# Latent attention: the order of the first value product, a two-bank value projection, and the rotated query's copies

## The chip, the cores and the metric

The kernel runs on one core of one Trainium2 chip. Its engines work side by side, each in its own order: TensorE (PE in the profile; its weight loads are PEld), VectorE (DVE), ScalarE (ACT), GpSimd (POOL) and SyncE (SP), which issues the transfers. The metric is the device time of one execution in microseconds; the time before is the median of three runs.

## The reference

Two layers of a decoder trunk over 512 tokens of width 1024, in float32. Each layer normalises its input, projects it once, and feeds three branches: a state-space scan (SSD), multi-head latent attention (MLA), and a gated delta network (GDN). Their outputs are gated, projected, and followed by a feed-forward block. The change lies in the MLA branch, whose core is, cut to what matters:

```python
q = (rmsnorm(cq, q_norm_g) @ w_uq).reshape(Bsz, S, H, MLA_NOPE + MLA_ROPE)   # 8 heads, 128 + 64
q_nope, q_pe = jnp.split(q, [MLA_NOPE], axis=-1)
q_pe = apply_rope(q_pe, ...)
kv = (rmsnorm(ckv, kv_norm_g) @ w_ukv).reshape(Bsz, S, H, MLA_NOPE + MLA_V)
k_nope, v = jnp.split(kv, [MLA_NOPE], axis=-1)
k_pe = apply_rope(k_rope, cos, sin)          # one rotated key of 64, shared by all heads
scale = (128 + 64) ** -0.5
# per block of 128 queries: scores = (q_nope . k_nope + q_pe . k_pe) * scale, causal,
# softmax over the keys, then the product with v
```

## The kernel before

Every large product is made of three matmuls on values split in two: a rounded high part (`h`) and the rest, the low part (`l`); high times high, high times low, low times high. ACT rounds the high part (L270, `split_act`), and DVE subtracts it from the source to get the low part (L271). Weights are split the same way (L170 on ACT, L171 on DVE) as they arrive. A scheduler sets the order on every engine from its own estimate of when operands are ready; products of later work ("fillers") are put between the steps of a head that wait for another engine. Results stand in eight PSUM banks of 128x512: four `acc`, three `sm`, one `yt`.

The attention takes the eight heads in four pairs (`hp`), two heads (`j`) in each:

- L589 to L608: the query weights are loaded and split, and the query product gives three banks: the plain queries of the two heads, and one bank with the rotated 64 columns of both (64 partitions each). For the first pair the third bank is `yt`.
- L610 to L627: the queries are split; the rotated part is scaled into `qp` and rotated by `rope` (L545 to L554). That makes a swapped copy by four transfers of 32 partitions (L549), then two products and a sum on DVE (L551 to L553).
- L629 to L636: the rotated query is needed twice over the 128 partitions, since its partner `kps` holds the high half of the rotated key in the first 64 partitions and the low half in the last 64. Two transfers of 64 partitions (L630) make a copy `qd` with the halves swapped. For each head ACT rounds its own half (L634) and the other half from `qd` (L636) into `qps[j]`, and DVE makes the low part `qpl[j]` (L635). The other half of `qpl[j]` is zeroed once (L585), so that it can be multiplied with the whole of `kph`.
- L637 to L639: key/value weights and the key product, `k`, two banks.
- L641 to L656: the value product for both heads, tokens on the partitions, into four `acc` banks of 128x256, one for each block of 128 tokens. Each bank is read out in two halves of 128x128, by ACT and by DVE.
- L658 to L681, for each head and each block `t` of 128 queries: five matmuls of scores (L667 to L671; L670 takes `qps`, L671 `qpl` with `kph`), then the softmax: DVE L676, ACT L678, DVE L679 and L680, into `pn`.
- L682 to L706: the probabilities are transposed on PE by key block `kb` (L688), split into `th` and `tl`, and multiplied into `po` (bank `yt`): L704 high values with `th`, L705 high values with `tl`, L706 low values with `th`. For `kb` 0, `th` and `tl` are 512 wide.
- L708: the head's output is split.

At the start of the branch L561 to L568 rotate the shared key and make `kph` and `kps`; `latent` (L274 on ACT, L275 on DVE) normalises and splits the latent `ckh`, `ckl`.

Of the kernel before, what the change touches and what calls it, by code (L numbers as in the profile page):

```python
# [10 lines left out]
F32 = mybir.dt.float32  # L11
# [44 lines left out]
def hybrid_kernel(ctx, tc, a, out, depth=2, taps=None):  # L56
# [4 lines left out]
    def mk(pl, shape, dt, tag, bufs=None):  # L61
        return pl.tile(shape, dt, tag=tag, name=f"{tag}_{next(uid)}", bufs=bufs)
# [5 lines left out]
    def f32(ap):  # L68
        return ap.bitcast(F32)
# [198 lines left out]
    def split_act(hi, lo, src):  # L268
        with tc.high_priority(30):
            act.copy(hi, src)  # L270
            dve.tensor_tensor(lo, src, f32(hi), ALU.subtract)  # L271
# [113 lines left out]
    for ly in range(depth):  # L385
# [177 lines left out]
        kpe = rope(kd)  # L563
        kph = mk(ml, [P, S], F32R, "kph")
        kps = mk(ml, [P, S], F32R, "kps")
        act.copy(kph, kpe)
        act.copy(kps[:64], kpe[:64])
        dve.tensor_tensor(kps[64:], kpe[64:], f32(kph[64:]), ALU.subtract)  # L568

# [10 lines left out]
        for x in pts:  # L580
            pool.memset(f32(x[:, :P]), 0.0)

        qpl = [mk(ml, [P, S], F32R, f"qpl{j}") for j in range(2)]
        for j in range(2):
            pool.memset(f32(qpl[j][64 * (1 - j) : 64 * (1 - j) + 64]), 0.0)  # L585

        scale = (128 + 64) ** -0.5
        yh, yl = [None] * KD, [None] * KD
        for hp in range(4):  # L589
# [37 lines left out]

            qd = mk(lp, [P, S], F32, "mix", 8)
            for i in range(2):  # L629
                sync.dma_start(qd[64 * i : 64 * i + 64], qr[64 * (1 - i) : 64 * (1 - i) + 64])  # L630
            qps = [mk(ml, [P, S], F32R, f"qps{j}") for j in range(2)]
            for j in range(2):
                half, other = (slice(64 * i, 64 * i + 64) for i in (j, 1 - j))
                act.copy(qps[j][half], qr[half])  # L634
                dve.tensor_tensor(qpl[j][half], qr[half], f32(qps[j][half]), ALU.subtract)  # L635
                act.copy(qps[j][other], qd[other])  # L636
            wkv = list(weights(a["mla_w_ukv"][ly], hp * 512, 512, 256))  # L637
# [4 lines left out]
            for j in range(2):  # L642
                if hp % 2 == 0:
                    v2 = [mk(ml, [P, S], F32R, nm, 2) for nm in ("vh", "vl")]
                elif hp == 1:
                    v2 = [mk(lp, [P, S], F32R, f"y{e}{6 + j}") for e in "hl"]
                else:
                    v2 = [mk(ml, [P, S], F32R, f"cq{e}{j}") for e in "hl"]
                vs.append([x.rearrange("p (t n) -> p t n", t=T) for x in v2])

            def ev(t, ps):
                for j in range(2):
                    split_act(*(x[:, t, :] for x in vs[j]), ps[:, j * P : (j + 1) * P])

            vcols = lambda w: w.rearrange("p (h n) -> p h n", h=2)[:, :, P:]
            dense_T(wkv, 256, 256, ckh, ckl, ev, vcols)  # L656

            for j in range(2):  # L658
# [3 lines left out]
                for t in range(T):  # L662
# [7 lines left out]
                    pe.matmul(o, qps[j][:, tok], kps[:, :n], start=False, stop=False)  # L670
                    pe.matmul(o, qpl[j][:, tok], kph[:, :n], start=False, stop=True)  # L671
                    n = (t + 1) * P
# [10 lines left out]
                for kbs in ((0,), (1,), (3, 2)):  # L683
# [16 lines left out]
                    for kb, c0, c in parts:  # L700
                        v_h, v_l = (x[:, kb, :] for x in vs[j])
                        o = po[:, c0:]
                        w = S - c0
                        pe.matmul(o, v_h, th[:, c : c + w], start=kb == 0, stop=False)  # L704
                        pe.matmul(o, v_h, tl[:, c : c + w], start=False, stop=False)  # L705
                        pe.matmul(o, v_l, th[:, c : c + w], start=False, stop=kb == T - 1)  # L706
# [800 lines left out]
```

## Time and profile before

| | us |
|---|---|
| median of three runs | 2264.68 (2264.63 to 2265.31) |
| the profiled execution, its own time | 2266.44 |
| its span | 2264.7 |
| PE busy | 2250.4 (99%) |
| DVE busy | 1648.5 (73%) |
| ACT busy | 1185.7 (52%) |
| POOL busy | 64.7 (3%) |

The granted clock of PE is 0.999 of full speed. The span is what the trace covers; the execution's own time has a little more around it. Times inside the trace count from the start of the span. The attention of the first layer lies at 58 to 210 us, that of the second at 1180 to 1340 us. A row of a timeline gives start, duration, engine, line, operation, written tile and read tiles, and shape; brackets give the idle time of the engine ahead of it and what ended it. An `x2` joins two operations.

### The profile page before, as it was taken

To read this page: it belongs to the slowest core of one execution; us is meant where nothing else is said; L and a number is where in the kernel's file an instruction comes from. 1 tells how busy PE (TensorE), PEld (TensorE's weight loads), DVE (VectorE), ACT (ScalarE), POOL (GpSimd) and SP (SyncE) were. 2 spreads that over 40 slices of the span, in tenths; PEclk is the share of its full clock that TensorE was granted. 3 is DMA by queue.
4 is the path that set the end of the run, shared out by engine and by line. 5 is a ranking of instruction groups with operands and counts; after the bars stand their busy time and mean duration, and the time that the engine had idled before them with its cause. 6 is when DMAs were issued, how large, how long until landed. Compare 5 with 4: busy or idle time off the path is not lost.

```text
span 2264.7 us, 32107 instructions
## 1 busy us (share of the span) xinstructions
PE 2250.4 (99%) x11758; PEld 1866.1 (82%) x11758; DVE 1648.5 (73%) x3315; ACT 1185.7 (52%) x2448; POOL 64.7 (3%) x84
## 2 busy tenths in 40 slices
PE   9999999999999999999999999999999999999998
PEld 8888787888888888888888887888888888888887
DVE  7886567876767778767878865678758668778668
ACT  6665644333543555554656667443335435645546
POOL 1000000000000000000010000000001000000000
PEclk9999999999999999999999999999999999999999
DMA  4223633452225143233132236345422251432231
GB/s 144 82 75 104 195 103 121 137 143 75 77 73 177 56 149 112 93 103 112 48 105 81 70 116 201 94 121 148 123 77 82 66 182 42 167 112 100 87 112 47
DMA packets 220030, 244.07 MB, mean 108 GB/s; under 512 B 34256, under 2 KB 172384, under 8 KB 219872
## 3 DMA queue, kind: packets, MB, share of 16 engines
q1 hardware_dynamic: 219728, 241.76, 34.7%
q8 instruction: 92, 1.51, 0.3%
q14 instruction: 66, 0.54, 0.1%
q10 hardware_dynamic: 144, 0.26, 0.0%
HBM read 225.53 MB, written 11.74 MB: 105 GB/s over the span
## 4 chain that ended last, share of the span: by engine, by line
PE 93%; DVE 3%; ACT 1%; DMA 1%; issue 0%; POOL 0%; SPq 0%; POOLq 0%; DVEq 0%; ACTq 0%
PE acc L198 24%; PE acc L202 24%; PE acc L201 24%; PE sm L201 2%; PE sm L202 2%; PE sm L198 2%; DVE wlo L171 1%; PE sm L688 1%; PE yt L704 1%; PE sm L792 1%; PE sm L1074 1%; PE sm L1100 1%; PE sm L803 1%; PE yt L198 1%; PE yt L201 1%; PE yt L202 1%
## 5 line engine op out<-in xcount | busy, mean ns | idle before, releaser
L171 DVE TENSOR_TENSOR wlo<-wraw,whi 128x512 fp32r<-128x512 f32 (+1 forms) x536 | 365.2, 686 | 328.3 <-ACT whi L170 317.2
L170 ACT CAST whi<-wraw 128x512 fp32r<-128x512 f32 (+1 forms) x536 | 329.5, 617 | 509.7 <-PE acc L201 336.9
L198 PE MATMUL acc<-xh,whi 128*128 128x512 f32 (+1 forms) x1344 | 524.5, 391 | 0.0
L202 PE MATMUL acc<-xh,wlo 128*128 128x512 f32 (+1 forms) x1344 | 520.7, 388 | 0.7 <-DVE wlo L171 0.7
L201 PE MATMUL acc<-xl,whi 128*128 128x512 f32 (+1 forms) x1344 | 518.7, 386 | 0.0
L202 PEld LDWEIGHTS acc<-xh,wlo 128*128 128x128 f32 x1344 | 252.4, 188 | 50.7 <-DVE wlo L171 1.5
L201 PEld LDWEIGHTS acc<-xl,whi 128*128 128x128 f32 x1344 | 252.6, 188 | 48.4 <-DVE xl L275 0.7
L198 PEld LDWEIGHTS acc<-xh,whi 128*128 128x128 f32 x1344 | 252.4, 188 | 48.3 <-ACT xh L274 0.4
L170 ACT CAST whi<-wr 128x512 fp32r<-128x512 f32 x168 | 104.3, 621 | 109.6 <-PE acc L201 47.4
L198 PE MATMUL acc<-yh,whi 128*128 128x512 f32 x384 | 152.3, 400 | 0.0
L201 PE MATMUL acc<-yl,whi 128*128 128x512 f32 x384 | 150.5, 392 | 0.0
L202 PE MATMUL acc<-yh,wlo 128*128 128x512 f32 x384 | 150.3, 391 | 0.0
L171 DVE TENSOR_TENSOR wlo<-wr,whi 128x512 fp32r<-128x512 f32 x168 | 113.2, 688 | 35.5 <-ACT whi L170 34.5
L729 DVE SCALAR_TENSOR_TENSOR ckl<-acc,pc,ckl 128x511 f32<-128x511 f32 (+2 forms) x168 | 120.9, 744 | 19.0 <-ACT ckl L725 10.6
L198 PEld LDWEIGHTS acc<-yh,whi 128*128 128x128 f32 x384 | 71.5, 188 | 16.1 <-ACT yh L274 2.3
L202 PEld LDWEIGHTS acc<-yh,wlo 128*128 128x128 f32 x384 | 72.1, 188 | 14.8
L201 PEld LDWEIGHTS acc<-yl,whi 128*128 128x128 f32 x384 | 72.2, 188 | 14.1
L198 PE MATMUL acc<-whi,xh 128*128 128x512 f32 (+1 forms) x208 | 80.0, 384 | 0.3
L202 PE MATMUL acc<-whi,xl 128*128 128x512 f32 (+1 forms) x208 | 79.3, 381 | 0.0
L201 PE MATMUL acc<-wlo,xh 128*128 128x512 f32 (+1 forms) x208 | 79.3, 381 | 0.0
L1220 DVE TENSOR_TENSOR h<-h,acc 128x512 f32<-128x512 f32 x120 | 77.1, 682 | 0.1
L488 ACT ACTIVATE eE<-eE,cum 128x128 f32<-128x128 f32 x192 | 63.2, 390 | 24.7 <-DMA eE<-d_c 20.8
(470 smaller groups left out, 4500.4 us busy)
## 6 DMA issues: line engine op xcount, KB each, us to landing
wraw<-in_w_in_dram SPq DMA_DIRECT2D x144, 512.0 KB, 3.6
wraw<-in_w_up_dram SPq DMA_DIRECT2D x64, 512.0 KB, 3.6
wr<-in_w_down_dram SPq DMA_DIRECT2D x32, 1024.0 KB, 5.0
eE<-d_c SPq DMA_DIRECT2D x48, 256.0 KB, 4.3
wraw<-in_w_mla_out_dram SPq DMA_DIRECT2D x16, 512.0 KB, 3.3
eE<-d_e SPq DMA_DIRECT2D x32, 256.0 KB, 3.0
wraw<-in_w_ssd_out_dram SPq DMA_DIRECT2D x16, 512.0 KB, 3.3
wraw<-in_w_gdn_out_dram SPq DMA_DIRECT2D x16, 512.0 KB, 3.4
```

The source lines that it names most:

```text
L170: act.copy(hi, raw)
L171: dve.tensor_tensor(lo, raw, f32(hi), ALU.subtract)
L198: x = pe.matmul(o, ah, bh, start=start, stop=False, skip_group_check=more)
L201: pe.matmul(o, ah, bl, start=False, stop=False, skip_group_check=more)
L202: return pe.matmul(o, al, bh, start=False, stop=stop, skip_group_check=more)
L488: act.activation(o[:, i], o[:, i], AF.Relu, scale=-1.0, bias=cum[:, t, h0 + i : h0 + i + 1])
L688: pe.transpose(ps[:, n : n + P], pn[t][:, kb * P : (kb + 1) * P], ident)
L704: pe.matmul(o, v_h, th[:, c : c + w], start=kb == 0, stop=False)
L729: dve.scalar_tensor_tensor(acc[:, d:], ps[:, : S - d], taps_[3 - d], acc[:, d:], ALU.mult, ALU.add)
L792: x = pe.matmul(py[64 * i : 64 * i + 64, c * P : (c + 1) * P], xd[:, t, h * 64 : (h + 1) * 64], e2[h // 4][:, h % 4, :], start=True, stop= ...
L803: pe.matmul(po[:, c * P : (c + 1) * P], st[:, c * P : (c + 1) * P], ctl[:, tok], start=True, stop=True)
L1220: place((tag, n, t), dve.tensor_tensor(hs_, hs_, ps[t], op))
```

## The change

It has four parts.

1. The first value product of a head (`kb` 0) takes `tl` before `th`; the three products are the same. The other key blocks keep their order.
2. The value product writes two whole banks: token blocks 0 and 1 side by side in the first, 2 and 3 in the second. Its matmuls are the same in number and size. Each bank is split by one 128x512 operation on ACT and one on DVE.
3. The rotated query is rounded once, 128x512, on ACT (`qph`), and DVE makes one low part `qpl` of 128x512. `qps[0]` and `qps[1]` are then filled by four transfers of 64 partitions from `qph`, with no copies on ACT.
4. In place of the zeroed halves of `qpl[j]`, the rotated key has two copies `kz[0]` and `kz[1]`, each with one half zero. This makes one more 64x512 copy on ACT ahead of the latent.

```diff
-        kph = mk(ml, [P, S], F32R, "kph")
+        kz = [mk(ml, [P, S], F32R, f"kz{j}") for j in range(2)]
         kps = mk(ml, [P, S], F32R, "kps")
-        act.copy(kph, kpe)
+        for j in range(2):
+            half, other = (slice(64 * i, 64 * i + 64) for i in (j, 1 - j))
+            pool.memset(f32(kz[j][other]), 0.0)
+            act.copy(kz[j][half], kpe[half])
         act.copy(kps[:64], kpe[:64])
-        dve.tensor_tensor(kps[64:], kpe[64:], f32(kph[64:]), ALU.subtract)
+        dve.tensor_tensor(kps[64:], kpe[64:], f32(kz[1][64:]), ALU.subtract)
...
-        qpl = [mk(ml, [P, S], F32R, f"qpl{j}") for j in range(2)]
-        for j in range(2):
-            pool.memset(f32(qpl[j][64 * (1 - j) : 64 * (1 - j) + 64]), 0.0)
...
-            qd = mk(lp, [P, S], F32, "mix", 8)
-            for i in range(2):
-                sync.dma_start(qd[64 * i : 64 * i + 64], qr[64 * (1 - i) : 64 * (1 - i) + 64])
+            qph, qpl = (mk(ml, [P, S], F32R, nm) for nm in ("qph", "qpl"))
+            act.copy(qph, qr)
+            dve.tensor_tensor(qpl, qr, f32(qph), ALU.subtract)
             qps = [mk(ml, [P, S], F32R, f"qps{j}") for j in range(2)]
             for j in range(2):
-                half, other = (slice(64 * i, 64 * i + 64) for i in (j, 1 - j))
-                act.copy(qps[j][half], qr[half])
-                dve.tensor_tensor(qpl[j][half], qr[half], f32(qps[j][half]), ALU.subtract)
-                act.copy(qps[j][other], qd[other])
+                for i in range(2):
+                    sync.dma_start(f32(qps[j][64 * i : 64 * i + 64]), f32(qph[64 * j : 64 * j + 64]))
...
-            def ev(t, ps):
-                for j in range(2):
-                    split_act(*(x[:, t, :] for x in vs[j]), ps[:, j * P : (j + 1) * P])
-
             vcols = lambda w: w.rearrange("p (h n) -> p h n", h=2)[:, :, P:]
-            dense_T(wkv, 256, 256, ckh, ckl, ev, vcols)
+            pss = [acc_bank() for _ in range(2)]
+            for k, wh, wl in wkv:
+                for t in range(T):
+                    tok = slice(t * P, (t + 1) * P)
+                    o = pss[t // 2][:, t % 2 * 256 : t % 2 * 256 + 256]
+                    ah, al, bh, bl = ckh[k][:, tok], ckl[k][:, tok], vcols(wh[:, 0, :]), vcols(wl[:, 0, :])
...
+                    pe.matmul(o, ah, bl, start=False, stop=False, skip_group_check=more)
+                    pe.matmul(o, al, bh, start=False, stop=k == 1, skip_group_check=more)
+            for v2, ps in zip(vs, pss):
+                split_act(*v2, ps)
+            vs = [[x.rearrange("p (t j n) -> p t j n", t=2, j=2) for x in v2] for v2 in vs]
...
-                    pe.matmul(o, qpl[j][:, tok], kph[:, :n], start=False, stop=True)
+                    pe.matmul(o, qpl[:, tok], kz[j][:, :n], start=False, stop=True)
...
-                        v_h, v_l = (x[:, kb, :] for x in vs[j])
+                        v_h, v_l = (x[:, kb % 2, j, :] for x in vs[kb // 2])
...
-                        pe.matmul(o, v_h, th[:, c : c + w], start=kb == 0, stop=False)
-                        pe.matmul(o, v_h, tl[:, c : c + w], start=False, stop=False)
+                        first, second = (tl, th) if kb == 0 else (th, tl)
+                        pe.matmul(o, v_h, first[:, c : c + w], start=kb == 0, stop=False)
+                        pe.matmul(o, v_h, second[:, c : c + w], start=False, stop=False)
                         pe.matmul(o, v_l, th[:, c : c + w], start=False, stop=kb == T - 1)
```

The line numbers behind these places move: the value product is L655, L659 and L660, the scores L674 to L678, the transposes L695, the value products of a head L712 to L714, the query weights' loads L592, the new transfers L633. The new operands let the scheduler put work in another order. Three places follow; names in the rows are written tile, then read tiles, with buffer numbers.

PE at the first value product of head 0 in layer 0, before (the last three transposes, then the products; `mix_926` is the high half of the probabilities, `mix_927` the low):

```order
L688 MATMUL sm_944<-ct_75,pn_205_914 128x128
L688 MATMUL sm_944<-ct_75,pn_201_901 128x128
L688 MATMUL sm_944<-ct_75,pn_205_914 128x128
L202 MATMUL acc_1210<-ckh_137_656,wlo_1202 128x512
L704 MATMUL yt_920<-mix_926,vh_820 128x512
L201 MATMUL acc_1209<-ckl_140_659,whi_1205 128x512
L202 MATMUL acc_1104<-cqh_92_455,wlo_1155 128x512
L202 MATMUL acc_1209<-ckh_138_657,wlo_1206 128x512
L705 MATMUL yt_920<-mix_927,vh_820 128x512
L706 MATMUL yt_920<-mix_926,vl_821 128x512
```

And after (`mix_912` is now the low half, `mix_911` the high):

```order
L695 MATMUL sm_929<-ct_75,pn_203_899 128x128
L695 MATMUL sm_929<-ct_75,pn_199_886 128x128
L695 MATMUL sm_929<-ct_75,pn_203_899 128x128
L202 MATMUL acc_1193<-ckh_139_661,wlo_1190 128x512
L201 MATMUL acc_1089<-cql_96_459,whi_1139 128x512
L198 MATMUL acc_1194<-ckh_139_661,whi_1189 128x512
L202 MATMUL acc_1089<-cqh_92_455,wlo_1140 128x512
L201 MATMUL acc_1194<-ckl_141_663,whi_1189 128x512
L712 MATMUL yt_905<-mix_912,vh_819 128x512
L713 MATMUL yt_905<-mix_911,vh_819 128x512
L714 MATMUL yt_905<-mix_911,vl_820 128x512
L712 MATMUL yt_905<-mix_922,vh_819 128x384
```

One product of other work stood between transposes and first value product, three between the first and the second; now five stand ahead of the first, and the three value products follow one another.

PE at the fourth bank of the value product, pair 0 of layer 0, before (`acc_824` to `acc_827` are the four banks; the brackets name semaphores waited for):

```order
L198 MATMUL acc_825<-whi_794,ckh_138_657 128x256
L201 MATMUL acc_825<-wlo_795,ckh_138_657 128x256
L202 MATMUL acc_825<-whi_794,ckl_140_659 128x256
L198 MATMUL acc_826<-whi_794,ckh_138_657 128x256
L198 MATMUL acc_827<-whi_790,ckh_137_656 128x256 [waits DVE_49]
L201 MATMUL acc_827<-wlo_791,ckh_137_656 128x256
```

And after, with two banks:

```order
L655 MATMUL acc_823<-whi_789,ckh_138_660 128x256
L659 MATMUL acc_823<-wlo_790,ckh_138_660 128x256
L660 MATMUL acc_823<-whi_789,ckl_140_662 128x256
L655 MATMUL acc_824<-whi_789,ckh_138_660 128x256 [waits DVE_49]
L659 MATMUL acc_824<-wlo_790,ckh_138_660 128x256
```

The last new wait on DVE in this product now stands at the second bank, six matmuls after the product's start; the fourth bank's, two thirds of the way through, is gone.

SP around the rotated query of pair 0, before (`mix_777` is the swapped copy `qd`):

```order
L593 DMA wraw_1466<-in_mla_w_uq_dram 128x2x384 [waits DMAHW1_49,DVE_49,Activation_49]
L630 DMA mix_777<-mix_773 64x512 [waits DVE_49,PE_49]
L630 DMA mix_777<-mix_773 64x512
L593 DMA wraw_1498<-in_mla_w_uq_dram 128x2x384 [waits DMAHW6_49,DMAHW2_49,DVE_49]
L177 DMA wraw_1560<-in_mla_w_ukv_dram 128x2x512 [waits DMAHW3_49,DMAHW7_49,DVE_49,Activation_49]
```

And after:

```order
L633 DMA qps_170_781<-qph_777 64x512 [waits Activation_49]
L633 DMA qps_170_781<-qph_777 64x512
L633 DMA qps_171_782<-qph_777 64x512 [waits DMAHW2_49]
L633 DMA qps_171_782<-qph_777 64x512 [waits DMAHW3_49]
L592 DMA wraw_1468<-in_mla_w_uq_dram 128x2x384 [waits DMAHW6_49,DMAHW4_49,DVE_49]
L177 DMA wraw_1529<-in_mla_w_ukv_dram 128x2x512 [waits DMAHW7_49,DMAHW5_49,DVE_49]
```

Two transfers that waited for DVE became four that wait for ACT's rounding, with the same weight loads behind them.

More of the change, by code (lines that the diff above doesn't have):

```diff
@@ L648, in hybrid_kernel @@
                     v2 = [mk(ml, [P, S], F32R, f"cq{e}{j}") for e in "hl"]
-                vs.append([x.rearrange("p (t n) -> p t n", t=T) for x in v2])
-            def ev(t, ps):
-                for j in range(2):
-                    split_act(*(x[:, t, :] for x in vs[j]), ps[:, j * P : (j + 1) * P])
+                vs.append(v2)
             vcols = lambda w: w.rearrange("p (h n) -> p h n", h=2)[:, :, P:]
-            dense_T(wkv, 256, 256, ckh, ckl, ev, vcols)
+            pss = [acc_bank() for _ in range(2)]
[4 more added lines that the diff above has]
+                    ah, al, bh, bl = ckh[k][:, tok], ckl[k][:, tok], vcols(wh[:, 0, :]), vcols(wl[:, 0, :])
+                    more = t % 2 == 1
+                    x = pe.matmul(o, ah, bh, start=k == 0 and not more, stop=False, skip_group_check=more)
+                    if k == 0 and more:
+                        after_product(x.ins, opened)
+                    opened = x.ins
+                    pe.matmul(o, ah, bl, start=False, stop=False, skip_group_check=more)
[3 more added lines that the diff above has]
+            vs = [[x.rearrange("p (t j n) -> p t j n", t=2, j=2) for x in v2] for v2 in vs]
             for j in range(2):
```

## The prediction

> **What bounds the kernel now.** I read first the page's busy shares and its chain of waits, then the two stretches of the span in which the changed code runs.
>
> ```profile
> PE 2250.4 (99%) x11758; PEld 1866.1 (82%) x11758; DVE 1648.5 (73%) x3315; ACT 1185.7 (52%) x2448; POOL 64.7 (3%) x84
> PE 93%; DVE 3%; ACT 1%; DMA 1%; issue 0%; POOL 0%; SPq 0%; POOLq 0%; DVEq 0%; ACTq 0%
> 58.00:210.00 152.00, 150.88 (x819) 126.15 (x818) 123.13 (x315) 102.38 (x256) 1.01 (x1) 1.00 0.30 87
> 1180.00:1340.00 160.00, 159.56 (x864) 134.08 (x863) 126.11 (x318) 105.43 (x260) 1.01 (x1) 1.00 0.31 88
> ```
>
> TensorE (PE) is busy for 99% of the span and makes 93% of the chain. The two attention stretches (the last two rows: stretch, length, then the busy time of PE, its weight loads, DVE, ACT) look the same, at full clock. The change keeps every matmul, so it can only win the moments in which PE stands still there. These are few, and a busy matmul hides part of them: the honest measure is the distance between two starts against the pace. At full pace a 128x512 matmul starts 0.227 us after the one before, a 128x256 matmul 0.12 us (rows below: 134.29 to 134.51, 67.75 to 67.87). The waits of PE in the first attention stretch, and the total of idle time ahead of the first value products (the row under their line), both layers:
>
> ```profile
> PE acc L201 <- DVE ckl L275: 0.5, 1, 0.5
> PE acc L198 <- DVE kl L271: 0.3, 1, 0.3
> PE sm L670 <- ACT qps L636: 0.2, 1, 0.2
>   ACT mix L270: 4.0, 14
>   PE sm L670: 0.6, 3
> ```
>
> The first three are PE's named waits in layer 0. The fourth says that the product line L704 stood idle 14 times, 4.0 us in all, for the high probabilities that ACT rounds. The fifth is from the view of the tile `qps`: PE's row of it, three waits of L670 in both layers. So there are four places; I take them in turn.
>
> **1. The first value product (4.0 us).** Head 0 of layer 0, from the timeline:
>
> ```profile
> 82.90 0.71 PE L688 MATMUL sm<-ct,pn 128*128 128x128 f32 x5
> 83.21 0.59 ACT L270 CAST mix<-sm 128x512 fp32r<-128x512 f32 x1
> 83.37 0.48 PE L202 MATMUL acc<-ckh,wlo 128*128 128x512 f32 x1
> 83.83 0.69 DVE L271 TENSOR_TENSOR mix<-sm,mix 128x512 fp32r<-128x512 f32 x1 [0.44 <-ACT mix L270]
> 83.85 0.50 PE L704 MATMUL yt<-mix,vh 128*128 128x512 f32 x1
> 84.19 0.39 PE L201 MATMUL acc<-ckl,whi 128*128 128x512 f32 x1
> 84.90 0.55 DVE L271 TENSOR_TENSOR mix<-sm,mix 128x384 fp32r<-128x384 f32 x1
> ```
>
> Call the start of the last five transposes z (82.90). One filler product follows them (83.37), then L704. Filler to L704 takes 0.48 instead of 0.227, and L704 to the next 0.34: together 0.37 us late. Some 0.09 of it follows any run of transposes, as the first matmul after one shows elsewhere (an estimate from 57.20 to 57.52, row in part 4), and stays. What is left, 0.28, times 14 is the group row's 4.0 us. The high probabilities are ready at z+0.90 (83.21+0.59), the low ones at z+1.62 (83.83+0.69).
>
> After the change the first product takes the low ones, so it may start only at z+1.62, or z+1.67 with the 0.05 us that a release takes here (83.80 to 83.85). But the order now stands differently: five 512-wide fillers between transposes and product in place of one (the rows shown with the change). PE's supply is 0.47 for the transposes, 0.09, and 5 x 0.227: it arrives at z+1.70. On heads 0, 2 and 6 that is a margin of 0.03 us; on the others, by the same count of the rows, supply is z+1.73 (heads 1, 3), 1.86 (head 4), 1.90 (head 7) and 2.58 (head 5). So the wait is covered, barely. What is late next is the second block's low product: its low probabilities end at z+2.55 (84.90+0.55), and PE, now with three products in a row and the next block's high product ahead, gets there at 1.70+3x0.227+0.175 = z+2.55, or 0.12 later on the heads where a score product stands between. I charge 0.05 us and a restart of 0.10 (the restart is seen in part 3) on about half of some 20 such close calls in two layers, that is 1.4 us. Gain: 4.0 - 1.4 = **2.6 us**; bounds 1.0 (every call misses) and 4.0 (none does).
>
> **2. The rotated query's copies (1.7 us at stake).** Head pair 2 of layer 0:
>
> ```profile
> 129.86 0.69 DVE L553 TENSOR_TENSOR mix<-mix,mix 128x512 f32<-128x512 f32 x1
> 130.61 2.10 SPq L630 DMA_DIRECT2D mix<-mix  x2
> 130.69 0.62 ACT L170 CAST whi<-wraw 128x512 fp32r<-128x512 f32 x1 [1.47 <-PE acc L201]
> 134.45 0.62 ACT L636 CAST qps<-mix 64x512 fp32r<-64x512 f32 x1 [0.28 <-DMA mix<-mix]
> 134.29 0.39 PE L201 MATMUL acc<-cql,whi 128*128 128x512 f32 x1
> 134.51 0.39 PE L202 MATMUL acc<-cqh,wlo 128*128 128x512 f32 x1
> 135.12 0.39 PE L670 MATMUL sm<-kps,qps 128*128 128x256 f32 x1 [0.21 <-ACT qps L636]
> 135.34 0.28 PE L671 MATMUL sm<-kph,qpl 128*128 128x256 f32 x1
> DMA to landing us min/median/max: 2.2/2.8/3.6
> DMA to landing us min/median/max: 2.0/3.0/4.3
> ```
>
> L670 starts 0.61 us after its predecessor, 0.38 over pace, and the next follows 0.10 late: 0.48 us. Pairs 1 and 2 of both layers read so, 1.7 us in sum (the profile names three of the four, 0.6 us of plain idle). Before, the chain is the rotation's last sum (L553, done 130.55), two transfers, two ACT copies. Now: L553, one ACT copy of 128x512 (0.62), four transfers, no copy behind. In pair 2 ACT must still finish its weight cast (131.31) first, so the copy runs 131.2 to 131.8; SP issues at 131.9 and, about 0.55 later, 132.4 (L630's issues are some 0.5 to 0.6 each). With the landing times of L630 (the first of the two landing rows) the second piece is there at 134.6, 135.2 or 136.0. PE arrives at about 135.3, since the new order puts about 0.6 us more of other products ahead (matmul rows between the two places times their pace). Stall 0, 0 or 0.75 us. In pair 1 the evictions that are gone from DVE bring L553 about 1.1 us forward, and about 1.05 us fewer products stand ahead, so that one stays even. Pairs 0 and 3 keep slack. Gain taken: **1.0 us**, bounds 0 and 1.7.
>
> Each pair now costs SP two more issues, 1.1 us, and the next weight load behind them starts that much later. It is hidden by the load's own wait for a free buffer, as here:
>
> ```profile
> 132.81 7.84 SPq L177 DMA_DIRECT2D wraw<-in_w_in_dram  x2
> ```
>
> Two loads, 7.84 us, nearly all of it waiting; without that cover it would be at most 1.1 us for each of 8 pairs. The second landing row above is of the rotation (L549), which sends four pieces in a row: 4.3 us at worst, against 3.6 for the pairs of L630; what that would do here is a rival below.
>
> **3. The value product's fourth bank (0.88 us).**
>
> ```profile
> 67.75 0.28 PE L202 MATMUL acc<-whi,ckl 128*128 128x256 f32 x1
> 67.87 0.28 PE L198 MATMUL acc<-whi,ckh 128*128 128x256 f32 x1
> 68.49 0.38 PE L198 MATMUL acc<-whi,ckh 128*128 128x256 f32 x1 [0.34 <-DVE kl L271]
> 68.71 0.28 PE L201 MATMUL acc<-wlo,ckh 128*128 128x256 f32 x1
> 1190.99 0.68 PE L198 MATMUL acc<-whi,ckh 128*128 128x256 f32 x2
> 1191.51 0.28 PE L201 MATMUL acc<-wlo,ckh 128*128 128x256 f32 x1
> ```
>
> In pair 0 the fourth bank still holds the second key half until DVE has split it. 67.87 to 68.49 is 0.62, 0.50 over pace, and 0.10 for the restart; in layer 1 two matmuls take 0.52 instead of 0.24. Sum 0.88. With two banks for all four token blocks, the product takes those that the queries left, read out long before. What waits next is the next pair's third query bank, on the eviction of the first value bank: four 128x512 operations in place of sixteen 128x128 ones, done an estimated 1.7 us before PE needs it. Gain **0.9 us**, bounds 0.4 (the wait moves to the copies of pair 0, which land about when PE comes) and 0.9.
>
> The evictions themselves:
>
> ```profile
> L271 DVE TENSOR_TENSOR vl<-acc,vh 128x128 fp32r<-128x128 f32 x16 | 3.9, 285 | 0.1
> L271 DVE TENSOR_TENSOR kl<-acc,kh 128x512 fp32r<-128x512 f32 x8 | 5.5, 687 | 0.4 <-ACT kh L270 0.4
> ```
>
> A pair's 8 low halves go from 8x0.285 = 2.3 us on DVE to 2x0.687 = 1.4; ACT drops three of its four copies of 0.62 (134.45). This lies beside PE's work and I cost it at nothing.
>
> **4. The latent's low half (loss).**
>
> ```profile
> 57.20 0.48 PE L198 MATMUL acc<-cqh,whi 128*128 128x512 f32 x1
> 57.52 0.40 PE L201 MATMUL acc<-cql,whi 128*128 128x512 f32 x1
> 58.76 1.28 ACT L274 ACTIVATE ckh<-sm,pc 128x512 fp32r<-128x512 f32 x2
> 59.92 1.41 DVE L275 SCALAR_TENSOR_TENSOR ckl<-sm,pc,ckh 128x512 fp32r<-128x512 f32 x2
> 60.72 0.50 PE L201 MATMUL acc<-ckl,whi 128*128 128x512 f32 x1 [0.47 <-DVE ckl L275]
> ```
>
> The zero-padded keys add one ACT copy (0.5 us) ahead of L274, and the order moves one 512-wide filler from before L201 to behind it. DVE starts on the low half at 59.92, when it is free, so the ACT copy hides; the filler's 0.23 shows, with rounding **-0.3 us**, in layer 0 alone (layer 1 has no such wait). Bounds 0 and -0.75 (copy and filler).
>
> **Sum.** 2.6 + 1.0 + 0.9 - 0.3 = 4.2 us. The profiled execution has a span of 2264.7 us and a time of 2266.4; the median of the runs, 2264.7, equals the span, so I subtract from it: **2260.5 us**, -0.19%. About 0.2% (4.5 us) is what a measurement of this kernel can tell from no change, so this stands at the edge.
>
> **Rivals.**
> *All of it.* The margins of part 1 hold on every head and the copies are always in time: 4.0 + 1.7 + 0.9 = 6.6, so 2258.1 us. For it: the margins come from many alike heads, DVE is less loaded after. Against: three heads of eight have 0.03 us.
> *The stalls only move.* The low product stalls on most heads (1.0 left of 4.0), the copies keep their wait (0), 0.4 from the banks, -0.75 at the latent: 0.7 us, so 2264.0 us.
> *Four transfers in a row are slow.* If the first pair of pieces shares the queue with the second and takes 4.3 instead of 2.8 us, pair 2's copy is there at 132.4+4.3 = 136.7, 1.4 us after PE; pair 1's about 1.2 us after. With restarts that is 2x(1.5+1.3) = 5.6 us where 1.7 stood: a loss of 3.9, and 2.6+0.9-0.3-3.9 = -0.7 gives 2265.4 us, slower than before. It decides from a landing time of some 3 us on. Against it: L630's pairs never took more than 3.6, and the median over the rotation's fours is 3.0. [...]
> *The low half comes late.* DVE works in order. On five heads of eight the new order puts a weight split (0.4 to 0.69 us, itself behind an ACT cast of up to 0.62, as in row 130.69) or an eviction between the softmax and the low half. If DVE is not free by z+0.93, each of these ten heads waits 0.69 to 1.31 us, 10 in all at 1.0 each; 4.2 - 10 gives 2270.5 us. Against it: DVE idles 0.44 us there now, and at 123 us of 152 it has room.
>
> **Chances.** Forecast (a gain of 3 to 5.5 us) 0.50; all of it 0.22; stalls only move 0.16; slow transfers 0.06; late low half 0.06. Faster by over 0.2%: the second case and 0.22 of the first, 0.44. Slower by over 0.2%: the last case and a little, 0.08. Within: 0.48. The range runs from 2257.8, just below "all of it", to 2264.2, which takes in the moved stalls and leaves out the two slow cases; the forecast's own is 2259.2 to 2261.7.
>
> **What would show it.** The row of idle time ahead of the first value product should fall from 4.0 us to 1.5 or less, now under DVE's low half; the score product that reads `qps` should wait for a transfer, if at all, in pair 2, for 0.5 us at most; no wait at the value product in pair 0; the wait at the latent's low half 0.2 to 0.3 longer. PE's matmul count stays 11758. Wrong would be: a wait of over 0.3 us on most first products, landings beyond 3.6 us, or a new wait outside the attention stretches.

## The result, and the profile after

The changed kernel takes 2261.13 us (median of 17 runs, 2259.84 to 2263.41), beside 2265.65 us for the kernel before (17 runs, 2264.58 to 2266.93). The ratio is 0.998, with a 95% interval of 0.9974 to 0.9987: 4.5 us or 0.20% faster, 0.6 us from the forecast. The forecast started from 2264.68 us, the median of the three runs before; beside the changed kernel the same program measures 1 us more, and the gain is 0.3 us larger than forecast. As the experiments show, the total came out nearer than its terms.

The page of the changed kernel (busy times; shares of the chain), then the two attention stretches with the columns as before:

```profile
PE 2246.2 (99%) x11758; PEld 1867.3 (83%) x11758; DVE 1638.1 (72%) x3259; ACT 1167.3 (52%) x2378; POOL 65.7 (3%) x84
PE 93%; DVE 3%; ACT 1%; DMA 1%; issue 1%; POOL 0%; SPq 0%; POOLq 0%; ACTq 0%; DVEq 0%
58.00:210.00 152.00, 149.94 (x820) 127.28 (x819) 117.02 (x285) 93.48 (x223) 1.12 (x1) 0.99 0.33 95
1180.00:1340.00 160.00, 159.72 (x875) 135.90 (x874) 121.62 (x291) 96.17 (x225) 1.12 (x1) 1.00 0.34 95
```

DVE and ACT have about 10 and 18 us less to do, as many matmuls run as before, and PE still makes the chain. The waits of PE, layer 0 first (three rows), then layer 1 (one row), and last the idle time ahead of the first value product's line (PE and its weight loads together):

```profile
PE acc L198 <- ACT ckh L274: 1.0, 1, 1.0
PE sm L677 <- DMA qps<-qph: 0.6, 1, 0.6
PE acc L201 <- DVE ckl L275: 0.5, 1, 0.5
PE sm L677 <- DMA qps<-qph: 0.2, 1, 0.2
  DVE mix L271: 1.9, 8
```

Gone are the waits on the copies by ACT and on the key's eviction. New are one at the latent (1.0 us) and one on the transfers, and the row of the first value product has halved. Head 0 of layer 0 now:

```profile
85.12 0.71 PE L695 MATMUL sm<-ct,pn 128*128 128x128 f32 x5
85.59 0.48 PE L202 MATMUL acc<-ckh,wlo 128*128 128x512 f32 x1
86.60 0.39 PE L201 MATMUL acc<-ckl,whi 128*128 128x512 f32 x1
86.83 0.46 PE L712 MATMUL yt<-mix,vh 128*128 128x512 f32 x1
87.13 0.40 PE L713 MATMUL yt<-mix,vh 128*128 128x512 f32 x1
87.36 0.39 PE L714 MATMUL yt<-mix,vl 128*128 128x512 f32 x1
```

L712 starts 1.71 us after the transposes began, exactly at the pace of the five fillers, and 0.23 after the last of them: no stall. What is left is 0.07 us behind it (0.30 to L713 instead of 0.23).

The new wait on the transfers stands in pair 3, which the forecast had given slack (SP's issues, then PE, then the landing times of those of the 32 pieces for which the trace has one, 19):

```profile
161.10 0.37 SPq L177 DMA_DIRECT2D wraw<-in_w_in_dram  x1
161.55 2.41 SPq L633 DMA_DIRECT2D qps<-qph  x4
165.64 0.39 PE L202 MATMUL acc<-xh,wlo 128*128 128x512 f32 x1
166.58 0.36 PE L677 MATMUL sm<-kps,qps 128*128 128x256 f32 x1 [0.55 <-DMA qps<-qph]
166.78 0.28 PE L678 MATMUL sm<-kz,qpl 128*128 128x256 f32 x1
DMA to landing us min/median/max: 2.2/2.4/4.4
```

L677 is 0.71 us over pace (0.94 less 0.23), and the restart costs 0.08. In layer 1 the same place is 0.41 late. The median piece lands after 2.4 us, but the pieces of pair 3, behind a weight load of 512 KB that is issued 0.45 us ahead of the first, after 3.6 to 4.4. The other new loss is at the latent (ACT, PE, DVE):

```profile
52.73 1.25 ACT L569 CAST kz<-mix 64x512 fp32r<-64x512 f32 x2 [1.88 <-DVE mix L553]
54.01 0.62 ACT L570 CAST kps<-mix 64x512 fp32r<-64x512 f32 x1
59.72 0.69 ACT L274 ACTIVATE ckh<-sm,pc 128x512 fp32r<-128x512 f32 x1
59.05 0.39 PE L202 MATMUL yt<-cqh,wlo 128*128 128x512 f32 x1
60.46 0.50 PE L198 MATMUL acc<-ckh,whi 128*128 128x512 f32 x1 [1.01 <-ACT ckh L274]
61.46 0.50 PE L201 MATMUL acc<-ckl,whi 128*128 128x512 f32 x1 [0.50 <-DVE ckl L275]
60.66 1.40 DVE L275 SCALAR_TENSOR_TENSOR ckl<-sm,pc,ckh 128x512 fp32r<-128x512 f32 x2
```

ACT reaches L274 at 59.72 instead of 58.76. From the last query product (59.05) to the second wait's end (61.46) PE takes 2.41 us for 0.45 us of work, 1.96 over pace; before it was 60.72 - 59.11 = 1.61 for three matmuls, 0.93 over pace. So 1.0 us is lost here, where the forecast had 0.3.

Right behind this, this one execution ran for 3.4 us at half speed (PE, then the stretch with the granted clock in the second column from its last but one, 0.52):

```profile
62.25 0.39 PE L198 MATMUL acc<-ckh,whi 128*128 128x512 f32 x1
63.17 0.63 PE L202 MATMUL acc<-cqh,wlo 128*128 128x512 f32 x1
63.60 0.63 PE L198 MATMUL acc<-cqh,whi 128*128 128x512 f32 x1
62.50:66.00 3.50, 3.50 (x10) 2.74 (x9) 0.79 (x2) 0.60 (x1) 0.00 (x0) 0.52 0.30 108
```

A 128x512 matmul starts 0.43 us after the last there instead of 0.23. Eight of them cost 1.6 us. The profiled execution took 2263.41 us, the slowest of the 17, so 1.6 of its time must be left out when it is compared.

To compare profiles I use two stretches of equal work: from the start of the 254th matmul to that of the 1251st (layer 0's attention and what is interleaved with it) and from the 6001st to the 7201st (layer 1's). All kernels run the same 11758 matmuls. Medians are set against the kernel before in the same set of runs.

| kernel | layer 0 | layer 1 | sum, against before | median, against before | ratio, interval |
|---|---|---|---|---|---|
| before | 186.57 | 222.72 | | | |
| changed | 186.58 (185.0 without the half-speed part) | 220.27 | -2.4 (-4.0) | -4.5 | 0.998 (0.9974 to 0.9987) |
| order of the first product alone | 185.48 | 221.17 | -2.6 | -3.1 | 0.9986 (0.9977 to 0.9995) |
| two banks alone | 184.40 | 221.01 | -3.9 | -3.3 | 0.9986 (0.9977 to 0.9995) |
| copies alone | 187.85 | 223.91 | +2.5 | +2.1 | 1.0007 (0.9999 to 1.0016) |
| changed, old product order | 186.56 | 221.81 | -0.9 | -1.2 | 0.9994 (0.9985 to 1.0003) |
| changed, old copies | 184.20 | 220.75 | -4.3 | -4.4 | 0.9982 (0.9973 to 0.9991) |
| two banks, small evictions | 186.08 | 222.12 | -1.1 | -1.5 | 0.9994 (0.9985 to 1.0003) |
| changed, half of kps by transfer | 184.10 | 220.12 | -5.1 | -5.4 | 0.9976 (0.9966 to 0.9986) |
| changed, load behind the transfers | 184.04 | 219.96 | -5.3 | -6.1 | 0.9973 (0.9962 to 0.9984) |
| both of these | 183.76 | 219.78 | -5.8 | -5.8 | 0.9974 (0.9964 to 0.9984) |
| both, and DVE rounds the query | 184.11 | 220.12 | -5.1 | -5.2 | 0.9978 (0.9969 to 0.9987) |
| changed, two more ACT copies | 186.88 (185.3) | 220.19 | -2.2 (-3.8) | -4.4 | 0.9981 (0.9972 to 0.9990) |

The intervals are up to 2.5 us to either side. A difference of 1 us or less between two changed kernels rests on the stretches and the waits in them, not on the medians.

### The profile page after: what moved, and what is told of

The parts are those of the page before. It is cut to its first block, busy times and chain, and to the rows that moved or that the text cites. A ratio compares the mean times of both kernels' runs of the same rounds, so it can differ in the third digit from the quotient of the medians.

```text
span 2261.6 us, 32000 instructions
## 1 busy us (share of the span) xinstructions
PE 2246.2 (99%) x11758; PEld 1867.3 (83%) x11758; DVE 1638.1 (72%) x3259; ACT 1167.3 (52%) x2378; POOL 65.7 (3%) x84
## 4 chain that ended last, share of the span: by engine, by line
PE 93%; DVE 3%; ACT 1%; DMA 1%; issue 1%; POOL 0%; SPq 0%; POOLq 0%; ACTq 0%; DVEq 0%
PE acc L198 24%; PE acc L202 23%; PE acc L201 23%; PE sm L202 3%; PE sm L198 3%; PE sm L201 3%; DVE wlo L171 1%; PE sm L695 1%; PE sm L1082 1%; PE sm L800 1%; PE yt L202 1%; PE yt L198 1%; PE yt L201 1%; PE sm L1108 1%; DVE ckl L737 1%
## 5 line engine op out<-in xcount | busy, mean ns | idle before, releaser
L201 PE MATMUL acc<-xl,whi 128*128 128x512 f32 (+1 forms) x1344 | 519.1, 387 | 0.0
L201 PEld LDWEIGHTS acc<-xl,whi 128*128 128x128 f32 x1344 | 252.9, 188 | 48.2 <-DVE xl L275 0.7
L201 PE MATMUL acc<-yl,whi 128*128 128x512 f32 x384 | 150.7, 392 | 0.0
L201 PEld LDWEIGHTS acc<-yl,whi 128*128 128x128 f32 x384 | 72.2, 188 | 14.1
L201 PE MATMUL acc<-wlo,xh 128*128 128x512 f32 (+1 forms) x208 | 79.3, 381 | 0.0
```

The source lines that it names most:

```text
L201: pe.matmul(o, ah, bl, start=False, stop=False, skip_group_check=more)
```

## The experiments

### The parts, one at a time

**The order of the first value product alone**, in the kernel before:

```diff
-                        pe.matmul(o, v_h, th[:, c : c + w], start=kb == 0, stop=False)
-                        pe.matmul(o, v_h, tl[:, c : c + w], start=False, stop=False)
+                        first, second = (tl, th) if kb == 0 else (th, tl)
+                        pe.matmul(o, v_h, first[:, c : c + w], start=kb == 0, stop=False)
+                        pe.matmul(o, v_h, second[:, c : c + w], start=False, stop=False)
```

> The kernel before, with the first value product of each head taking the low probabilities, and nothing else changed. Theory (the swap is what moves other products ahead of the first value product): the idle time ahead of that product falls from 4.0 us to under 1 us, and the time is 3 to 4 us below before. Rival (the gain comes from fewer operations on ACT and DVE, which let the probabilities come earlier): within 1 us of before, and the idle time moves under DVE's low half.

Measured: 3.1 us below before (2261.93 beside 2265.01), 2.6 in the stretches. The theory holds, and with it the first term of the forecast. But the idle time ahead of the product's line did not fall under 1 us; it only changed its owner, as the rival had it:

```profile
  DVE mix L271: 3.2, 12
```

The row before was 4.0 for 14 times, under ACT. This row counts the idle time of the weight loads too, which here ends while PE still works (the row has 3.2 us, but no wait of PE at this line is named); by the starts of the matmuls the products' delays are halved, from 5.2 to 2.7 us over all heads with the matmul behind them. The row is a good pointer to a place and a poor measure of its price.

**Two banks alone:**

```diff
...
-            dense_T(wkv, 256, 256, ckh, ckl, ev, vcols)
+            pss = [acc_bank() for _ in range(2)]
...
+            for v2, ps in zip(vs, pss):
+                split_act(*v2, ps)
...
```

> The kernel before, with the value product in two banks and nothing else changed. Theory: PE's waits at the fourth bank go (0.5 + 0.1 us in layer 0, 0.3 us in layer 1), 0.9 us below before; the first value products still stand idle for 4 us. Rival (lighter evictions matter): 3 us or more below before.

Measured: 3.3 us below before, 3.9 in the stretches. The theory's 0.9 fails, and the rival's number stands. The first value products still wait as before (4.2 us in their row), so the gain is elsewhere: the waits on the rotated query's copies, which this kernel does not touch, have mostly gone. By the starts of the matmuls, the first score product on the copies is late by 1.70 us in sum before, restarts included, and by 0.38 us here.

The rotation itself does not come sooner against PE's work: in pair 1 of layer 0, PE starts 21 matmuls between the rotation's last sum and this product before, and 17 here. What is shorter is the way from that sum to the end of the last copy, 5.1 us before and 3.9 us here. SP and the landing time of this pair's transfers, before (three rows), then here:

```profile
100.73 0.39 SPq L593 DMA_DIRECT2D wraw<-in_mla_w_uq_dram  x1
101.35 1.15 SPq L630 DMA_DIRECT2D mix<-mix  x2
DMA to landing us min/median/max: 3.4/3.4/3.4
99.43 0.39 SPq L593 DMA_DIRECT2D wraw<-in_mla_w_uq_dram  x1
100.82 1.15 SPq L630 DMA_DIRECT2D mix<-mix  x2
DMA to landing us min/median/max: 2.5/2.5/2.5
```

The weight load of 384 KB is issued 0.6 us ahead of the transfers before, and 1.4 us ahead here. That this distance sets the landing time is only read from the rows here; an edit that moves a load from ahead of such transfers follows further down.

**Two banks, small evictions.** To tell the banks from the lighter evictions, the same two banks were read out in pieces as small as before:

```diff
             for v2, ps in zip(vs, pss):
-                split_act(*v2, ps)
+                for c in range(4):
+                    split_act(*(x[:, c * P : (c + 1) * P] for x in v2), ps[:, c * P : (c + 1) * P])
```

> The kernel before with the value product in two banks, as in the run with the banks alone, but each bank read out in four pieces of 128x128 on ACT and on DVE, as many operations as before the change. Theory (most of what the two banks gave came from the lighter evictions, which let DVE reach the query's rotation earlier): only the fourth bank's wait goes; the score product waits again on ACT's copies in pairs 1 and 2, 0.2 to 0.4 us each over pace; about 1 us below before. Rival (two banks in place of four are the whole gain, by the queries' and values' banks that come free earlier): 3 us below before, as with the large evictions, and no wait on the copies.

Measured: 1.5 us below before, 1.1 in the stretches. The theory's number holds. The idle row of the score product on the copies, in the kernel before, with small and with large evictions:

```profile
  ACT qps L636: 4.0, 11
```

```profile
  ACT qps L636: 3.0, 9
```

```profile
  ACT qps L636: 1.8, 6
```

By starts the delays are 1.70, 1.09 and 0.38 us. The waits left with small evictions stand in pair 0 of both layers and in pair 2 of layer 0, not in pairs 1 and 2 as the theory has it. So in the stretches about 1.1 us of the 3.9 goes with the banks and 2.8 with four 128x512 operations in place of sixteen 128x128 ones (in the medians 1.5 and 1.8). Some 0.7 of the 2.8 is the wait on the copies: in pair 0, with small evictions, the last copy stands on ACT behind a weight cast that waits for PE (two rows). The rest is spread over many small delays and is not traced.

```profile
75.47 0.41 ACT L601 CAST whi<-wraw 128x256 fp32r<-128x256 f32 x1 [0.45 <-PE acc L201]
75.90 0.62 ACT L636 CAST qps<-mix 64x512 fp32r<-64x512 f32 x1
```

**The copies alone** (the rotated query and key, without the banks and the new order):

```diff
...
-                act.copy(qps[j][half], qr[half])
-                dve.tensor_tensor(qpl[j][half], qr[half], f32(qps[j][half]), ALU.subtract)
-                act.copy(qps[j][other], qd[other])
+                for i in range(2):
+                    sync.dma_start(f32(qps[j][64 * i : 64 * i + 64]), f32(qph[64 * j : 64 * j + 64]))
...
```

> The kernel before, with the rotated query's and key's copies alone. Theory: the waits of the score product on its copies go in pairs 1 and 2 (1.7 us), new ones come in pair 3, where a weight load is issued ahead of the four transfers (1.2 us), and the latent is 1.1 us later: 0.6 us above before. Rival (the copies are a gain as costed in the forecast, 1.0 - 0.3): 0.7 us below before.

Measured: 2.1 us above before, 2.5 in the stretches; the interval of the median reaches from no change to 3.6 us. The sign is the theory's, the mechanism only in part. No score product waits for a copy in any pair, not in pair 3 either, where in this kernel the weight load is issued behind the four transfers (SP's rows) and they land after 2.4 us at most:

```profile
160.46 2.42 SPq L633 DMA_DIRECT2D qps<-qph  x4
162.98 0.53 SPq L177 DMA_DIRECT2D wraw<-in_w_in_dram  x1
```

Some of the waits of PE in layer 0:

```profile
PE acc L198 <- ACT ckh L274: 0.7, 1, 0.7
PE yt L701 <- ACT mix L270: 0.5, 1, 0.5
PE sm L761 <- DVE tok L283: 0.4, 1, 0.4
```

The latent's wait is there. The second row is a new one: on the second head of pair 2 the scheduler now puts no filler at all between the transposes and the first value product, which is 0.63 us late, and the one behind it 0.50; the same in layer 1. The third row is in the state-space branch behind the attention, 0.57 us over pace in layer 0 and 0.98 in layer 1. So these two losses stand where the new operands left another order of the fillers. For the second row that is seen in the order; for the third it is inferred.

**The changed kernel with the old product order:**

> The changed kernel with the old order of the first value product (high probabilities first). Theory: the first value products wait again, 4 us; the time is 3 to 4 us above the changed kernel, near before. Rival (evictions and copies carry the gain): within 1 us of the changed kernel, 4 us below before.

Measured: 1.2 us below before, so the order of the product is worth 3.3 us within the changed kernel, as alone. The theory holds. It also equals two banks and copies together (-3.3 + 2.1), while the wait in pair 3 is there (0.6 us by name in layer 0).

**The changed kernel with the old copies**, that is the new order and two banks only:

> The changed kernel's new product order and two value banks, with the rotated query's and key's copies as before the change. Theory (parts add up: the order is worth 3.1 us, the banks 3.3, the copies cost 2.1): 6.4 us below before, 2 us below the changed kernel; no wait on the copies, since the lighter evictions already bring the rotation forward. Rival (the copies gain once the rest is in place, since the fillers have moved): 4.5 us below before or less, with waits of the score product on ACT's copies of 0.3 us or more in pairs 1 and 2.

Measured: 4.4 us below before (2261.13 beside 2265.56), the same as the changed kernel. The theory of adding parts fails by 2 us; the rival's number stands, and in part its sign: of the waits on ACT's copies 0.8 us is left, in pairs 1 and 2. A gain of the copies does not show. What cost 2.1 alone costs nothing here. The waits of the copies alone, on a head without fillers and in the branch behind, are not among the waits of the changed kernel. So the third part of the change neither gains nor loses beside the other two: it takes 0.8 us of waits away and brings 1.3 in pair 3 and 1.0 at the latent, against smaller gains spread over the stretches.

### The two new losses

**Half of `kps` by a transfer:**

```diff
-        act.copy(kps[:64], kpe[:64])
+        sync.dma_start(f32(kps[:64]), f32(kz[0][:64]))
```

> The changed kernel with one edit: the first half of kps is filled by a transfer from kz[0] in place of an ACT copy, so that ACT has two 64x512 copies ahead of the latent, as many operations as before the change. Theory (the extra ACT copy delays the latent's high half, and with it PE, by 1.1 us in layer 0): PE's wait on ACT ckh in layer 0 falls from 0.7-1.0 us to under 0.2, time 1 us below the changed kernel. Rival (the order of the products, with one filler less ahead of the latent, makes the wait): the wait stays, time the same.

Measured: 5.4 us below before, 0.9 more than the changed kernel. PE at the latent:

```profile
59.49 0.51 PE L198 MATMUL acc<-ckh,whi 128*128 128x512 f32 x1 [0.22 <-ACT ckh L274]
60.70 0.50 PE L201 MATMUL acc<-ckl,whi 128*128 128x512 f32 x1 [0.70 <-DVE ckl L275]
```

The wait on ACT falls to 0.2, that on DVE rises to 0.7. From the last query product (58.88) it is 1.82 us for two matmuls, 1.37 over pace: 0.6 us better than the changed kernel's 1.96, 0.4 worse than before's 0.93. So some 0.6 us of the loss goes with ACT's extra copy. The rest stands with one filler less ahead, which I take for its cause. Theory and rival each hold in part. Not all of the 0.9 us lies here: the wait on the transfers in pair 3 is 0.2 us by name in this kernel, instead of 0.6.

**Two more ACT copies** ahead of the latent:

```diff
+        for _ in range(2):
+            act.copy(kps[:64], kpe[:64])
         query_latent(1)
```

> The changed kernel with two more 64x512 copies on ACT ahead of the latent, which write again what kps already holds. Theory (ACT's queue sets the latent's high half): PE waits 1.0 us longer for ckh in layer 0, time 1.0 us above the changed kernel. On the half-speed stretch of 3.3 us that the changed kernel's profile shows behind its wait at the latent: if the idle time of PE sets it off, it comes in this kernel's profile too and in most of its runs, and the time is 2.6 us above; if it is chance, it is absent.

Measured: 4.4 us below before, no slower than the changed kernel, where the theory had 1.0 more.

```profile
60.81 0.50 PE L198 MATMUL acc<-ckh,whi 128*128 128x512 f32 x1 [1.86 <-ACT ckh L274]
61.61 0.50 PE L201 MATMUL acc<-ckl,whi 128*128 128x512 f32 x1
62.00:65.50 3.50, 3.50 (x10) 2.72 (x9) 1.47 (x4) 1.20 (x3) 0.00 (x0) 0.51 0.37 112
```

The wait for the high half is 0.9 us longer, as expected, but PE then hardly waits for the low half: a filler is back between the two, and L201 starts at 61.61, 3.05 us after the last query product (58.56) with three matmuls in between, 2.37 over pace. That is 0.4 more than in the changed kernel, not 1.0. So a delay on ACT takes away part of the wait on DVE that follows. The half-speed stretch came again in this profile (last row), behind 1.86 us of idle time. But only 2 of 10 runs show the mean clock of 0.998 that goes with one, so idle time here does not set it off each time.

**The load behind the transfers.** In pair 3 of each layer the scheduler may not put the next weight load ahead of the first two pieces:

```diff
...
+        if copied:
+            copied[0] -= 1
+            if not copied[0]:
+                after_product(x.ins, copied[1])
+                copied.clear()
...
```

> The changed kernel with one edit: in pair 3 of each layer the weight load that stood ahead of the four transfers on SP is ordered behind the first two of them. Theory (the load, 512 KB issued 0.45 us earlier, makes the transfers land after 4.4 us): the first two land after 2.2 to 2.6 us, the score product's wait in pair 3 (0.71 and 0.41 us over pace) goes, 1.2 us below the changed kernel. Rival (four transfers in a row are slow in themselves there): landing stays at 4 us, and the wait stays.

Measured: 6.1 us below before, 1.6 more than the changed kernel; 1.3 in the stretches when the half-speed part is left out. SP and the landing times:

```profile
159.90 2.42 SPq L638 DMA_DIRECT2D qps<-qph  x4
162.41 3.55 SPq L177 DMA_DIRECT2D wraw<-in_w_in_dram  x2
DMA to landing us min/median/max: 2.2/2.3/2.5
```

With the load behind, no piece whose landing the trace has takes more than 2.5 us, and no score product waits. The theory holds: four transfers in a row are not slow here (2.5 us at most), and a load 0.45 us in front of them makes them slow (3.6 to 4.4 us in the changed kernel).

**Both edits**, and **DVE rounds the query** on top (`dve.tensor_copy(qph, qr)` in place of `act.copy(qph, qr)`):

> The changed kernel with both edits: half of kps by a transfer from kz[0], and in pair 3 the weight load behind the first two of the four transfers. Theory (two separate losses of the changed kernel, at the latent 0.3 to 1 us and in pair 3 1.2 us): 1.5 to 2 us below the changed kernel, 6 to 6.5 below before, no wait on the copies left. Rival (they are not separate, the delayed load or the freed ACT time only moves the stall): 5.4 to 6.1 us below before, as with either edit alone, with a wait of PE on a weight split behind pair 3.

> As the one before, and the rotated query is rounded on DVE, right behind the rotation's last sum, in place of ACT. Theory (ACT's weight casts and evictions stand ahead of the rounding by up to 1.3 us): the four transfers are issued about 0.5 to 1.3 us earlier in each pair; where nothing waits for them any more it changes nothing, so within 0.5 us of the one before. Rival (DVE is the busier engine and the extra 0.7 us comes ahead of the softmax and the low probabilities): 1 us or more above the one before, with waits on DVE at the first value products.

Measured: 5.8 and 5.2 us below before. With both edits the theory's 6 to 6.5 is not reached; the number is the rival's, but its wait on a weight split behind pair 3 does not show. The two losses hardly add in the medians (5.4, 6.1, 5.8); in the stretches both together are the shortest of all kernels (403.5 us beside 404.0 and 404.2), with no wait left on the copies. The median, 2259.10 us, is the lowest in this study, about 1.3 us better than the changed kernel against its own runs before (5.8 less 4.5), which is less than the intervals can tell. With the rounding on DVE nothing is gained: 0.5 us more in the medians and 0.7 in the stretches, between theory and rival, and no named wait accounts for it. The theory's earlier issue does not hold in each pair: counted from the rotation's last sum in layer 0, the transfers are issued 0.8 us sooner in pair 2 but 0.5 us later in pair 1.

## Why the prediction was right, and where it was not

The forecast of 2260.5 us, its range and its direction held. The terms did not all.

The signs named beforehand came in part. The idle row ahead of the first value product fell from 4.0 to 1.9 us, where 1.5 or less was forecast, but stands under DVE's low half; nothing waits at the value product in pair 0; the matmuls are 11758. The latent's low half waits 0.5 us as before, and the new wait, 1.0 us, is for its high half. The wait on a transfer stands in pair 3 and not in pair 2, and with 4.4 us a landing went beyond the 3.6 us that the prediction had named as a sign of being wrong.

1. **The first value product: 2.6 us forecast, 2.6 in the stretches and 3.1 in the median measured.** Right, with its reason: fillers move ahead, and the low probabilities are ready when PE arrives. The close calls that were charged 1.4 us cost about 1.0 by the starts. They stand at another place than forecast: most of it is 0.05 to 0.08 us behind the first product on twelve of the sixteen heads, and only 0.06 us, on four heads, at the second block.
2. **The copies: 1.0 us forecast, a loss of 2.1 alone and nothing beside the other two parts.** Two steps failed. "Pairs 0 and 3 keep slack" stands in the prediction without a sum, and the landing times that it takes over, 2.2 to 3.6 us, are those of L630. In pair 3 no load was issued for 7.8 us ahead of L630, and its pieces landed after 2.2 to 2.3 us. With one 0.45 us ahead the new ones took up to 4.4, and the wait came in pair 3: 0.79 us with its restart in layer 0, 0.48 in layer 1. Moving the load removed it. The rival of slow transfers had the right sort of delay, for another reason, in another pair. The 4.3 us of the rotation's fours (L549), on which it rested, can be read in the same way in the trace of the kernel before: with no load issued for 5.7 us ahead (66.01) they landed after 2.0 us, with one of 512 KB 0.46 to 0.48 us ahead (six places) after 2.8 to 4.3. And the 1.7 us at stake were not this part's alone to win: the two banks with lighter evictions take most of them (1.70 to 0.38 us). The same wait was counted once as a gain of the copies and, unseen, again as a gain of the banks.
3. **The banks: 0.9 us forecast, 3.3 alone.** The fourth bank's wait was right: 0.9 us by the starts before, and gone with either form of the two banks. The step that failed is "This lies beside PE's work and I cost it at nothing", of the evictions: with small evictions only 1.1 of the 3.9 us in the stretches is left. How they cost is shown in part only. Some 0.7 us of the 2.8 is the wait on the copies in pairs 0 and 2; the rest is not traced. In pair 1 the wait goes with either form of the two banks: its transfers land about 1 us sooner, with the weight load further ahead of them, and why the load moves is not traced either.
4. **The latent: -0.3 forecast, -1.0 measured.** "The ACT copy hides" failed: ACT reached the latent 1.0 us later, and 0.6 us of the loss went with the copy.

The sum was right because two errors cancelled, which is luck: copies and latent together were forecast at 0.7 us and give nothing, order and banks together at 3.5 and give 4.4. It also rests on an overlap that was not seen: alone, order and banks are worth 3.1 and 3.3 us, together 4.4. A part of the overlap is the wait on the copies, which the order alone shortens too: its idle row of 4.0 us falls to 2.5 with the order, 1.8 with the banks and 1.3 with both.

## What to carry to other kernels

Where two edits relieve the same engine or shorten the same chain, price them together: a wait can be cured only once. Operations that lie beside the busiest engine are not free for that: here four large evictions in place of sixteen small ones were worth 2.8 us in the stretches. Look at what is issued ahead of a small transfer; here a weight load 0.45 us ahead added up to 2 us (a landing after 4.4 us where the median is 2.4). And the order in which equal terms are accumulated can be used to let the scheduler see the later operand, so that it fills the gap.

## What was not expected of the hardware

In the kernels with the new transfers a piece of 64x512, 128 KB, landed after 2.2 to 2.7 us wherever no weight load was issued just ahead of it, also with four in a row (of the pieces whose landing the traces have). In the changed kernel it was 2.2 to 2.6 us in pairs 0 to 2, where the last weight load had been issued 2.0 us or more ahead of the first piece. In pair 3, behind a load of 512 KB issued 0.45 us ahead, it took 3.6 to 4.4 us there and 3.4 to 4.5 us over four kernels, in both layers.

PE ran for 3.4 us at half speed (62.66 to 66.07 us of the changed kernel's profile, granted clock 0.50, a 128x512 matmul every 0.43 us) behind idle times of 1.0 and 0.5 us within the 3.4 us before it, and, in the kernel with two more ACT copies, behind one of 1.9 us. In three other profiles (the copies alone, the old product order, the load behind the transfers) idle times of 0.7 and 0.5 us at the same place left the clock alone, at 0.999 in the mean. Idle time alone does not decide: in the changed kernel's profile PE is busy for 1.90 us in the 3.41 us from 59.25 to 62.66 us, ahead of the half speed, and just as long in the 3.42 us from 8.04 to 11.46, behind which the clock stayed full (1.00 from 11.46 to 14.90 us). Nor is a low mean clock peculiar to these kernels: 0.998 also stands with one run each of the kernel before, the order alone and the two banks alone, each time the slowest of its set. What sets the half speed off, and why some runs show the lower mean clock and most do not, stays open.
